# Small matrix products of two token mixers: HGRN scores gathered by tile width, meta blocks padded to full tiles, gated linear attention on blocks of 128 tokens

## The chip, the cores and the metric

The kernel runs on one core of a Trainium2 chip. The metric is device time in microseconds (us) of one execution, the median of three runs. Engines are named as in the profile: PE (TensorE matmul), PEld (its weight load), DVE (VectorE), ACT (ScalarE), POOL (GpSimd), SP (SyncE, which here only issues DMAs).

## The reference

Two transformer blocks run one after the other on 512 tokens of width 1024, all in float32. Both end in a gated feed-forward part of width 2816 with a short causal convolution. Ahead of that, the first block mixes tokens by gated linear attention (GLA, 4 heads of 128), a short convolution and sliding-window attention (SWA); the second, which has 16 learned meta tokens in front, by HGRN2 (8 heads of 128) and a Mamba-2 scan. The change touches GLA, HGRN2 and one transposition in Mamba-2.

GLA, per head, in chunks of 64 tokens (q, k already projected):

```python
b = jnp.cumsum(log_a, axis=2)                       # inside a chunk
attn = einsum('bnihk,bnjhk->bnhij', q * exp(b - b_ref), k * exp(b_ref - b))   # causal
o_intra = einsum('bnhij,bnjhv->bnihv', attn, v)
kv = einsum('bnjhk,bnjhv->bnhkv', k * exp(b_last - b), v)
state = exp(b_last) * state + kv                    # from chunk to chunk
o_inter = einsum('bnihk,bnhkv->bnihv', q * exp(b), state_before)
```

HGRN2 has the same form in chunks of 16, with a forget gate f in place of exp(log_a) and k = 1 - f:

```python
scores = where(causal, einsum('bnhrk,bnshk->bnhrs', q * exp(bcum), k * exp(-bcum)), 0)
o = einsum('bnhrs,bnshv->bnrhv', scores, v) + o_inter
```

## The kernel before

The large products stream through PE without a break: a weight tile of 128x128 times activations of 512 columns (256, 258 or 264 columns where meta tokens are carried along), in three passes, because each float32 operand is held as an exact sum of two parts (XH and XL, wh and wl). They write the PSUM tile `acc`. ACT (line 82) and DVE (line 83) make wh and wl of every eight weight tiles.

The token mixers are "small work" in three lanes: generators that are stepped after every k-step of the stream (`tick`). A `yield n` asks for n ticks before the next step. Their products write the PSUM tile `sm` and stand in PE's one queue between the large products; PE takes its queue in order. Which large products they stand between was set when the program was built, and is shown below where it changes. A float32 product of the mixers is two PE instructions ("passes") in the profile, a transposition one.

A product uses the part of the array that its operands need. The profile writes this as rows*columns: 128*128 is the whole array, 128*32 a product with 32 columns of weights, 32*128 one with 32 rows in the sum. Products that lie in different rows or columns of the array can be in flight side by side.

HGRN, `hg_head` and `hg_back`: the 528 tokens of a head are a meta block of 32 (16 zeros, 16 meta tokens) and four blocks of 128. Scores of a 128-block come in three steps: the whole block with factors taken relative to each sub-block of 32 (Km, Qm; in the profile `Qm,hb`), then two 32x32 corrections between neighbouring sub-blocks (K32, Q32), then a 64x64 correction (K64, Q64), each of which overwrites its part of PSUM. The `yield`s are at block level, so all of a head's score products are issued in one step. Then K and V are transposed to tokens (kt, vt), states S are summed (`kt` times `vt`, decays on DVE), outputs are at (scores) times vt plus Q1 times S, and the normed output `on` is transposed back. The meta block is a product with 32 rows (kt, vt, at0, on0). In Mamba-2's `z_gen`, the meta rows of `xtm` are transposed as a 16-row tile.

GLA, `gla_head`: chunks of 64 are paired into blocks of 128 columns. q1, k2 give the scores of a block (mask `glam` cuts it to two chunks); k4 is transposed to tokens; seven chunk products with 64 rows give seven states; outputs are at times v plus q3 times the state before, per chunk of 64.

Of the kernel before, what the change touches and what calls it, by code (L numbers as in the profile page):

```python
# [9 lines left out]
F32 = mybir.dt.float32  # L10
# [89 lines left out]
class Lane:  # L100
    """Small work that runs beside the stream of large matrix products."""
# [25 lines left out]
class Builder:  # L127
# [162 lines left out]
    def spread(self, cols, dst, pos=0):  # L290
        """cols: list of [n,1] token columns -> dst[:, pos:...] the same on all partitions."""
# [12 lines left out]
    def setup(self):  # L304
# [5 lines left out]
        cm = c.tile([P, 5 * P + 16], F32, name="cm")  # L310
        self.four = cm[:, 5 * P:]
        self.ident, self.le, self.gt, self.glam, self.ones = (cm[:, i * P:(i + 1) * P] for i in range(5))
# [30 lines left out]
    def swa(self, pool, sq, sk, svt):  # L343
        """Heads 0..3 live on the partitions 0..63, heads 4..7 on 64..127: one of each runs side by side."""
# [59 lines left out]
    def gla_head(self, pool, h, q, k, sgr):  # L404
# [25 lines left out]
        yield 8  # L430
# [4 lines left out]
        nc.vector.copy_predicated(at, self.glam.bitcast(U32).unsqueeze(1).to_broadcast([P, 4, P]), a4(ps))  # L435
        ebl = pool.tile([P, 8], F32, tag="ebl", name="ebl", bufs=2)
        nc.vector.tensor_copy(ebl, c3(q3)[:, :, 63])
        self.mul(k4, k4, k)
        self.mul(q3, q3, q)
# [7 lines left out]
        Ss = [None] + [None] * 7  # L447
        Sa, Sb = t2("q1"), pool.tile([P, 3, P], F32, tag="S", name="S", bufs=1)
        pks = [self.sm(), self.sm()]
        for n in range(7):  # L450
            blk, r = n // 2, (n % 2) * 64
            pk = pks[n % 2][:, n // 2 * P:(n // 2 + 1) * P]
            self.mm(pk, k4T[r:r + 64, blk * P:(blk + 1) * P], self.GVt[r:r + 64, blk, h * P:(h + 1) * P])
            Ss[n + 1] = a4(Sa)[:, n, :] if n < 4 else Sb[:, n - 4, :]
        for n in range(7):
            pk = pks[n % 2][:, n // 2 * P:(n // 2 + 1) * P]
            if n == 0:
                nc.vector.tensor_copy(Ss[1], pk)
            else:
                self.stt(Ss[n + 1], Ss[n], ebl[:, n:n + 1], pk, ALU.mult, ALU.add)  # L460
            if n == 3:
                yield 2
        yield 3
        po = self.sm()
        for n in range(8):
            blk, r = n // 2, (n % 2) * 64
            vb = self.GVt[:, blk, h * P:(h + 1) * P]
            if blk == 0:
                self.mm(po[r:r + 64, 0:P], at[:, 0, r:r + 64], vb, start=True, stop=r == 0)
            elif r == 0:  # L470
                self.mm(po[:, blk * P:(blk + 1) * P], at[:, blk, :], vb, start=True, stop=False)
            if n:
                self.mm(po[r:r + 64, blk * P:(blk + 1) * P], q3[:, n * 64:(n + 1) * 64], Ss[n], start=False, stop=True)
# [358 lines left out]
    def to_tokens(self, c, dst):  # L832
        """c [128, L] features -> dst [128, 5, 128] tokens, block 0 the meta tokens."""
# [88 lines left out]
    def hg_head(self, hp, h, f, hv, st, prev, back):  # L922
# [65 lines left out]
        p3 = ps.rearrange("p (a b) -> p a b", a=4)  # L988
        for i in range(4):
# [5 lines left out]
        at, at0 = self.hat, self.hat0  # L995
# [4 lines left out]
        ps0 = self.sm()  # L1000
        self.mm(ps0[0:32, 0:32], Km[:, 0:32], Qm[:, 0:32])
        nc.vector.copy_predicated(at0, self.le[0:32, 0:32].bitcast(U32), ps0[0:32, 0:32])
        self.mul(c3(Q1), c3(Qm), bc(fq, 17, 32))
        yield 1
        vt, kt = hp.tile([P, 5, P], F32, tag="hvt", name="hvt"), hp.tile([P, 5, P], F32, tag="hkt", name="hkt")
# [18 lines left out]
    def hg_back(self, hp, h, at, at0, Q1, kt, vt, tot, st):  # L1024
# [23 lines left out]
        nc.gpsimd.memset(ss, 0.0)  # L1048
        on, on0 = hp.tile([P, T], F32, tag="hon", name="hon"), hp.tile([32, P], F32, tag="hon0", name="hon0")
        self.act(on0, po0[0:32, 0:P], AF.Square, accum=ss[0:32, 0:1])  # L1050
# [6 lines left out]
        self.ts(on0, po0[0:32, 0:P], r[0:32, 0:1], ALU.mult)  # L1057
# [4 lines left out]
        self.tr(ps0[:, 0:32], on0, 32)  # L1062
# [6 lines left out]
    def block2(self, sqh, sqg):  # L1069
# [5 lines left out]
        def norm2():  # L1075
# [4 lines left out]
            # 1/sqrt(s2 r1^2 / D + EPS) r1 = 1/sqrt(s2 / D + EPS / r1^2)  # L1080
# [19 lines left out]
        with ExitStack() as sy:  # L1100
# [26 lines left out]
            with tc.tile_pool(reuse_waits="tile", name="m2", bufs=1) as mp:  # L1127
                xtm = mp.tile([P, 5, D], F32, name="xtm")
                Cs = [mp.tile([P, L], F32, name=f"mC{g}") for g in range(2)]
# [61 lines left out]
                def z_gen(j):  # L1191
# [8 lines left out]
                    self.tr(ps0[:, 0:META], xtm[0:META, 0, j * P:(j + 1) * P], META)  # L1200
# [68 lines left out]
            with tc.tile_pool(reuse_waits="tile", name="hp", bufs=1) as hp:  # L1269
# [6 lines left out]
                self.hat0 = hp.tile([32, 32], F32, name="hat0")  # L1276
                for a in (self.hat, self.hat0):
# [119 lines left out]
    def rms_spread(self, acc, dim, R, pos):  # L1397
        """acc [128, 2 + 512] sums of squares -> R[:, pos:...] the factor per column."""
# [10 lines left out]
def np_consts():  # L1409
# [4 lines left out]
    glam = le & (i[:, None] // 64 == i[None, :] // 64)  # L1414
    cm = np.concatenate([ident, le, gt, glam, np.ones((P, P)), i[:, None] % 32 == i[:16]], 1).astype(np.float32)
# [84 lines left out]
```

## Time and profile before

| what | us |
|---|---|
| three runs | 1825.75, 1828.38, 1829.14; median 1828.38 |
| profiled execution, first to last instruction (span) | 1825.3 |
| PE busy in the span | 1795.8 (98%) |
| DVE, ACT, POOL busy | 1120.1 (61%), 703.4 (39%), 173.1 (9%) |

The profile tells the span of its execution; the time of that execution lies a little above it, and the three runs lie 0.5 to 3.8 us above the span. Busy time of PE is a sum of intervals whose ends are modelled, so 98% says that something was always in flight, not that PE worked at its best pace. A row of the timeline merges like instructions that follow each other: its first number is the start of the first, and the distance from one row's start to the next tells what a group really cost.

### The profile page before, as it was taken

What the parts mean: (1) busy time and instruction counts of PE and PEld (TensorE: products, weight loads), DVE (VectorE), ACT (ScalarE), POOL (GpSimd) and SP (SyncE); (2) the same over time, 40 slices, a digit from 0 to 9 for tenths busy, and PEclk for the clock granted to TensorE, in tenths of its full rate; (3) what the DMA queues carried; (4) which work ended last, traced back from release to release, by engine and by line L of the source; (5) the groups of instructions that cost most, each with busy time, mean ns of one, the idle gap of its engine ahead of it and who ended that gap; (6) DMA issues with size and microseconds to landing.
All of it is one profiled execution on the core that took longest, in us unless ns stands there. A gap on an engine that the chain in (4) does not pass through costs nothing. (4 is left out here: it accounts for less than half of the span.)

```text
span 1825.3 us, 26947 instructions
## 1 busy us (share of the span) xinstructions
PE 1795.8 (98%) x11012; PEld 1559.1 (85%) x11012; DVE 1120.1 (61%) x1946; ACT 703.4 (39%) x1097; POOL 173.1 (9%) x231
## 2 busy tenths in 40 slices
PE   8999999999999999999999999999999999999997
PEld 6777778888888888888988889999999999999875
DVE  5476774444467777533698787666643577777332
ACT  5355342222344444333443334544432344444221
POOL 2000000000200000011154640000001000000000
PEclk9999999999999999999998999999999999999998
DMA  5221223233232223232211122121223233232222
GB/s 182 81 81 47 81 70 93 93 99 98 92 93 93 93 93 96 96 97 93 73 60 46 59 64 70 50 79 59 70 70 93 93 93 93 93 91 91 94 84 69
DMA packets 43451, 153.55 MB, mean 84 GB/s; under 512 B 5024, under 2 KB 5168, under 8 KB 43328
## 3 DMA queue, kind: packets, MB, share of 16 engines
q1 hardware_dynamic: 42480, 149.83, 26.1%
q8 instruction: 86, 1.41, 0.3%
q0 software_dynamic: 560, 1.74, 0.3%
q14 instruction: 37, 0.30, 0.1%
q10 hardware_dynamic: 288, 0.27, 0.0%
HBM read 149.72 MB, written 2.10 MB: 83 GB/s over the span
## 5 line engine op out<-in xcount | busy, mean ns | idle before, releaser
L179 PE MATMUL acc<-XH,wh 128*128 128x512 f32 (+3 forms) x2320 | 636.5, 328 | 0.0
L179 PE MATMUL acc<-XH,wl 128*128 128x512 f32 (+3 forms) x2320 | 620.7, 321 | 0.0
L179 PE MATMUL acc<-XL,wh 128*128 128x512 f32 (+3 forms) x2320 | 620.6, 321 | 0.0
L82 ACT CAST wh<-wraw 128x1024 fp32r<-128x1024 f32 (+1 forms) x279 | 291.9, 1046 | 538.9 <-PE acc L179 473.8
L83 DVE TENSOR_TENSOR wl<-wraw,wh 128x1024 fp32r<-128x1024 f32 (+1 forms) x279 | 343.2, 1230 | 214.5 <-ACT wh L82 207.0
L179 PEld LDWEIGHTS acc<-XH,wh 128*128 128x128 f32 x2320 | 385.9, 189 | 45.0 <-issue 8.8
L179 PEld LDWEIGHTS acc<-XH,wl 128*128 128x128 f32 x2320 | 385.9, 189 | 35.7 <-issue 1.8
L179 PEld LDWEIGHTS acc<-XL,wh 128*128 128x128 f32 x2320 | 386.3, 189 | 34.0 <-issue 0.9
L179 PE MATMUL acc<-FH,wh 128*128 128x512 f32 x352 | 140.5, 399 | 0.0
L179 PE MATMUL acc<-FH,wl 128*128 128x512 f32 x352 | 139.1, 395 | 0.0
L179 PE MATMUL acc<-FL,wh 128*128 128x512 f32 x352 | 138.2, 393 | 0.0
L162 DVE SCALAR_TENSOR_TENSOR c<-u,par_t,c 128x512 f32<-128x512 f32 x176 | 131.8, 749 | 6.8 <-ACT c L176 3.7
L150 DVE TENSOR_TENSOR u<-acc,R 128x512 f32<-128x512 f32 (+2 forms) x132 | 63.8, 510 | 90.1 <-PE acc L179 87.1
L334 POOL TENSOR_TENSOR sqa<-sqa,sqt 128x512 f32<-128x512 f32 x27 | 40.9, 1516 | 745.7 <-ACT sqt L176 745.7
L179 PEld LDWEIGHTS acc<-FH,wl 128*128 128x128 f32 x352 | 66.1, 188 | 16.8
L179 PEld LDWEIGHTS acc<-FL,wh 128*128 128x128 f32 x352 | 66.1, 188 | 15.7
L179 PEld LDWEIGHTS acc<-FH,wh 128*128 128x128 f32 x352 | 66.1, 188 | 14.9
L176 ACT ACTIVATE FH<-c 128x512 fp32r<-128x512 f32 x44 | 27.8, 632 | 116.3 <-DVE c L150 116.3
L150 DVE TENSOR_TENSOR H<-H,acc 128x512 f32<-128x512 f32 (+2 forms) x41 | 22.6, 568 | 77.8 <-PE acc L179 77.8
L176 ACT ACTIVATE c<-u,par_t 128x512 f32<-128x512 f32 x88 | 67.8, 770 | 2.2 <-DVE u L150 2.2
L176 ACT ACTIVATE c<-c 128x512 f32<-128x512 f32 x44 | 27.8, 632 | 85.7 <-DVE c L162 85.7
L179 PE MATMUL acc<-yh,wh 128*128 128x256 f32 (+1 forms) x256 | 51.5, 283 | 0.0
(388 smaller groups left out, 2087.4 us busy)
## 6 DMA issues: line engine op xcount, KB each, us to landing
wraw<-in_wts SPq DMA_DIRECT2D x277, 512.0 KB, 3.5
H<-in_xT SPq DMA_DIRECT2D x8, 256.0 KB, 9.0
out<-H SPq DMA_DIRECT2D x7, 256.0 KB, 2.7
wraw<-in_wts SPq DMA_DIRECT2D x2, 256.0 KB, 4.4
cm<-in_cm POOLq DMA_DIRECT2D x1, 328.0 KB, 5.7
r<-in_r POOLq DMA_DIRECT2D x1, 272.0 KB, 3.8
par_t<-in_par POOLq DMA_DIRECT2D x1, 256.0 KB, 4.0
r<-in_r POOLq DMA_DIRECT2D x1, 256.0 KB, 6.8
```

The costliest lines, as they stand in the source:

```text
L82: self.nc.scalar.copy(h[:, e], t[:, e])
L83: self.nc.vector.tensor_tensor(out=l[:, e], in0=t[:, e], in1=h[:, e].bitcast(F32), op=ALU.subtract)
L150: self.nc.vector.tensor_tensor(out=out, in0=a, in1=b, op=op)
L162: self.nc.vector.scalar_tensor_tensor(out=out, in0=a, scalar=s, in1=b, op0=op0, op1=op1)
L176: self.nc.scalar.activation(out=out, in_=a, func=func, scale=scale, **kw)
L179: self.nc.tensor.matmul(out, lhsT, rhs, start=start, stop=stop)
L334: self.nc.gpsimd.tensor_tensor(out=acc, in0=acc, in1=t, op=ALU.add)
```

## The change

Four edits. (1) HGRN scores: the four whole blocks first, then the eight 32x32 corrections, then the 64-corrections, each cut into two products with 32 columns of weights and 64 columns of data, so that all corrections have the width 128*32; the meta block's 32x32 product comes right behind. (2) Meta blocks are zero-padded to 128 rows: kt, vt, at0, on0 and the meta block of xtm are full tiles whose unused rows POOL zeroes once; the products and transpositions on them are 128*128. (3) GLA runs on blocks of 128: k4 and q3 are scaled by the decay of the neighbouring chunk, a separate product of 64x64 fills the scores between the two chunks of a block, three kv products of 128 rows replace seven of 64, three states seven, and seven output products of 128 replace twelve. (4) The mask glam is dropped from the constants. Comments and docstrings are removed too.

```diff
@@ gla_head
+        ebl = pool.tile([P, 12], F32, tag="ebl", name="ebl", bufs=2)
+        nc.vector.tensor_copy(ebl[:, 0:8], c3(q3)[:, :, 63])
+        e2 = ebl[:, 0:8].rearrange("p (n a) -> p n a", a=2)
+        eb = ebl[:, 8:12]
+        self.mul(eb, e2[:, :, 0], e2[:, :, 1])
+        self.mul(k4, k4, k)
+        self.mul(q3, q3, q)
+        yield 6
         ps = self.sm()
         for n in range(4):
             self.mm(ps[:, n * P:(n + 1) * P], k2[:, n * P:(n + 1) * P], q1[:, n * P:(n + 1) * P])
+        for n in range(4):
+            self.mm(ps[0:64, n * P + 64:(n + 1) * P], k4[:, n * P:n * P + 64], q3[:, n * P + 64:(n + 1) * P])
+        h2 = lambda t, a: t.rearrange("p (n a c) -> p n a c", a=2, c=64)[:, :, a, :]
+        self.mul(h2(k4, 0), h2(k4, 0), e2[:, :, 1:2].to_broadcast([P, 4, 64]))
+        self.mul(h2(q3, 1), h2(q3, 1), e2[:, :, 0:1].to_broadcast([P, 4, 64]))
...
-        for n in range(7):
-            blk, r = n // 2, (n % 2) * 64
-            pk = pks[n % 2][:, n // 2 * P:(n // 2 + 1) * P]
-            self.mm(pk, k4T[r:r + 64, blk * P:(blk + 1) * P], self.GVt[r:r + 64, blk, h * P:(h + 1) * P])
...
+        for n in range(3):
+            self.mm(pk[:, n * P:(n + 1) * P], k4T[:, n * P:(n + 1) * P], self.GVt[:, n, h * P:(h + 1) * P])
+        nc.vector.tensor_copy(S[:, 0, :], pk[:, 0:P])
+        for n in (1, 2):
+            self.stt(S[:, n, :], S[:, n - 1, :], eb[:, n:n + 1], pk[:, n * P:(n + 1) * P], ALU.mult, ALU.add)
...
+        for n in range(4):
+            c = slice(n * P, (n + 1) * P)
+            self.mm(po[:, c], at[:, n, :], self.GVt[:, n, h * P:(h + 1) * P], start=True, stop=n == 0)
             if n:
-                self.mm(po[r:r + 64, blk * P:(blk + 1) * P], q3[:, n * 64:(n + 1) * 64], Ss[n], start=False, stop=True)
+                self.mm(po[:, c], q3[:, c], S[:, n - 1, :], start=False, stop=True)
@@ hg_head
         for i in range(4):
             self.mm(p3[:, i, :], sc(Km, i), sc(Qm, i))
+        for i in range(4):
             for g in range(2):
                 self.mm(p3[64 * g:64 * g + 32, i, 64 * g + 32:64 * g + 64], K32[:, 2 * i + g, :], Q32[:, 2 * i + g, :])
-            self.mm(p3[0:64, i, 64:128], K64[:, 2 * i:2 * i + 2, :].rearrange("p a b -> p (a b)"),
-                    Q64[:, 2 * i:2 * i + 2, :].rearrange("p a b -> p (a b)"))
+        for i in range(4):
+            for g in range(2):
+                self.mm(p3[32 * g:32 * g + 32, i, 64:128], K64[:, 2 * i + g, :],
+                        Q64[:, 2 * i:2 * i + 2, :].rearrange("p a b -> p (a b)"))
+        ps0 = self.sm()
+        self.mm(ps0[0:32, 0:32], Km[:, 0:32], Qm[:, 0:32])
@@ hg_back
         for i in range(4):
-            n = 32 if i == 0 else P
-            self.mm(pk[:, i * P:(i + 1) * P], kt[0:n, i, :], vt[0:n, i, :])
+            self.mm(pk[:, i * P:(i + 1) * P], kt[:, i, :], vt[:, i, :])
...
-            n = 32 if i == 0 else P
-            o = po0[0:32, 0:P] if i == 0 else po[:, (i - 1) * P:i * P]
-            self.mm(o, at0 if i == 0 else at[:, i - 1, :], vt[0:n, i, :], start=True, stop=i == 0)
+            o = po0[:, 0:P] if i == 0 else po[:, (i - 1) * P:i * P]
+            self.mm(o, at0 if i == 0 else at[:, i - 1, :], vt[:, i, :], start=True, stop=i == 0)
...
-        self.tr(ps0[:, 0:32], on0, 32)
+        self.tr(ps0[:, 0:P], on0)
@@ block2
+                nc.gpsimd.memset(xtm[:, 0, :], 0.0)
...
-                    self.tr(ps0[:, 0:META], xtm[0:META, 0, j * P:(j + 1) * P], META)
+                    self.tr(ps0[:, 0:P], xtm[:, 0, j * P:(j + 1) * P])
```

PE's queue in the second HGRN head, before the change (the last number is the size of the output; `Qm,hb` is a whole block or, as 32x32, the meta block; `q,k` are the corrections):

```order
L179 MATMUL acc<-XH,wl 128x258
L179 MATMUL sm<-Qm,hb 128x128
L179 MATMUL sm<-q_9173,k_9174 32x32 x2
L179 MATMUL sm<-q_9175,k_9176 64x64
L179 MATMUL sm<-Qm,hb 128x128
...
L179 MATMUL sm<-Qm,hb 32x32
L179 MATMUL acc<-XH,wh 128x256
```

The first three `sm` rows stand four times, once for each block, so the width changes three times in each. After the change, at the same place:

```order
L179 MATMUL acc<-XH,wl 128x258
L179 MATMUL sm<-Qm,hb 128x128 x4
L179 MATMUL sm<-q_9147,k_9148 32x32 x8
L179 MATMUL sm<-q_9149,k_9150 32x64 x8
L179 MATMUL sm<-Qm,hb 32x32
L179 MATMUL acc<-XH,wh 128x256
```

The width now changes once on the way in and once on the way out, and there are four more products.

PE's queue at the outputs of the third GLA head before the change (`GVt,attnT` is at times v, `q,b` and `S,b` are the state times q3):

```order
L179 MATMUL sm<-GVt,attnT_162 64x128 x2
L179 MATMUL sm<-q_1833,b 64x128
L179 MATMUL sm<-GVt,attnT_162 128x128
L179 MATMUL sm<-q_1833,b 64x128 x2
L179 MATMUL sm<-GVt,attnT_162 128x128
L179 MATMUL sm<-q_1833,b 64x128
L179 MATMUL sm<-S,b 64x128
L179 MATMUL sm<-GVt,attnT_162 128x128
L179 MATMUL sm<-S,b 64x128 x2
```

After the change, from the scores of the same head on (`q,k` with a product of 128x128 are the scores, `b,la` is the new product between chunks, `cm,la` transposes k4, `GVt,a` is kv; "..." stands for 9, 6 and 9 large products):

```order
L179 MATMUL sm<-q_1707,k_1708 128x128 x4
L179 MATMUL sm<-b,la 64x64 x4
...
L182 MATMUL sm<-cm,la 128x128 x4
...
L179 MATMUL sm<-GVt,a_1791 128x128 x3
...
L179 MATMUL sm<-GVt,attnT_162 128x128 x2
L179 MATMUL sm<-q_1799,b 128x128
L179 MATMUL sm<-GVt,attnT_162 128x128
L179 MATMUL sm<-q_1799,b 128x128
L179 MATMUL sm<-GVt,attnT_162 128x128
L179 MATMUL sm<-q_1799,b 128x128
```

Everything but `b,la` has the full width now; `b,la` stands between two full-width groups.

## Rows read from the trace of the kernel before

**Rows 1.** The page: span, and PE's busy time.

```profile
span 1825.3 us, 26947 instructions
PE 1795.8 (98%) x11012; PEld 1559.1 (85%) x11012; DVE 1120.1 (61%) x1946; ACT 703.4 (39%) x1097; POOL 173.1 (9%) x231
```

**Rows 2.** What PE waited for: us in total, times, longest us.

```profile
PE sm L182 <- POOL xtm L918: 1.1, 1, 1.1
```

**Rows 3.** Windows: length, busy us of PE, PEld, DVE, ACT, POOL, clock, DMA.

```profile
200.00:400.00 200.00, 199.85 (x912) 159.35 (x911) 114.26 (x171) 68.81 (x98) 0.10 (x1) 1.00 0.28 89
...
900.00:1000.00 100.00, 92.45 (x658) 84.36 (x657) 90.00 (x146) 36.84 (x64) 43.63 (x43) 0.93 0.17 54
...
1200.00:1300.00 100.00, 100.00 (x828) 94.47 (x826) 63.39 (x177) 45.83 (x97) 3.69 (x19) 1.00 0.21 64
```

**Rows 4.** Timeline of PE (start us, us, instruction), scores of GLA's third head.

```profile
212.99 0.39 PE L179 MATMUL acc<-XH,wl 128*128 128x512 f32 x1
213.22 1.05 PE L179 MATMUL sm<-q,k 128*128 128x128 f32 x8
...
214.34 0.40 PE L179 MATMUL acc<-XL,wh 128*128 128x512 f32 x1
```

**Rows 5.** Timeline of PE, scores of one HGRN head.

```profile
1226.62 0.41 PE L179 MATMUL acc<-XH,wl 128*128 128x264 f32 x2
...
1227.62 0.49 PE L179 MATMUL sm<-Qm,hb 128*128 128x128 f32 x2
1228.04 0.51 PE L179 MATMUL sm<-q,k 128*32 128x32 f32 x6
...
1230.73 0.41 PE L179 MATMUL acc<-XL,wh 128*128 128x264 f32 x2
```

**Rows 6.** Timeline of PE, two halves of an SWA output.

```profile
153.48 0.32 PE L179 MATMUL sm<-pT,svt 128*64 128x128 f32 x1
153.49 0.32 PE L179 MATMUL sm<-pTb,svt 128*64 128x128 f32 x1
```

**Rows 7.** Timeline of PE, 16 passes of 64 columns in Mamba-2.

```profile
942.62 1.06 PE L179 MATMUL sm<-xdt,Lm 16*16 16x64 f32 x16
943.62 0.51 PE L179 MATMUL acc<-XH,wh 128*128 128x264 f32 x2
```

**Rows 8.** Timeline of PE, around the state products of one HGRN head.

```profile
1234.74 0.40 PE L179 MATMUL acc<-XL,wh 128*128 128x264 f32 x2
1234.98 0.40 PE L179 MATMUL acc<-XH,wl 128*128 128x264 f32 x2
...
1236.75 0.40 PE L179 MATMUL acc<-XL,wh 128*128 128x264 f32 x2
```

**Rows 9.** Timeline of PE, around the output products of that head.

```profile
1239.18 0.41 PE L179 MATMUL acc<-XH,wl 128*128 128x256 f32 x2
...
1241.98 0.40 PE L179 MATMUL acc<-XL,wh 128*128 128x256 f32 x2
```

**Rows 10.** Timeline of PE, around the transpositions of that head's output.

```profile
1251.65 0.40 PE L179 MATMUL acc<-XH,wl 128*128 128x256 f32 x2
...
1252.95 0.40 PE L179 MATMUL acc<-XL,wh 128*128 128x256 f32 x2
```

**Rows 11.** Timeline of PE, around kv of GLA's third head.

```profile
217.83 0.39 PE L179 MATMUL acc<-XH,wl 128*128 128x512 f32 x1
...
219.58 0.39 PE L179 MATMUL acc<-XL,wh 128*128 128x512 f32 x1
```

**Rows 12.** Timeline of PE, around the outputs of that head.

```profile
222.60 0.39 PE L179 MATMUL acc<-XH,wl 128*128 128x512 f32 x1
...
226.21 0.39 PE L179 MATMUL acc<-XL,wh 128*128 128x512 f32 x1
```

**Rows 13.** The page's groups: a DVE product and a POOL sum of 512 columns.

```profile
L334 POOL TENSOR_TENSOR sqa<-sqa,sqt 128x512 f32<-128x512 f32 x27 | 40.9, 1516 | 745.7 <-ACT sqt L176 745.7
...
L150 DVE TENSOR_TENSOR H<-H,acc 128x512 f32<-128x512 f32 (+2 forms) x41 | 22.6, 568 | 77.8 <-PE acc L179 77.8
```

More of the change, by code (lines that the diff above doesn't have):

```diff
@@ L309, in setup @@
         self.par_t = c.tile([P, NPAR], F32, name="par_t")
-        cm = c.tile([P, 5 * P + 16], F32, name="cm")
-        self.four = cm[:, 5 * P:]
-        self.ident, self.le, self.gt, self.glam, self.ones = (cm[:, i * P:(i + 1) * P] for i in range(5))
+        cm = c.tile([P, 4 * P + 16], F32, name="cm")
+        self.four = cm[:, 4 * P:]
+        self.ident, self.le, self.gt, self.ones = (cm[:, i * P:(i + 1) * P] for i in range(4))
         nc.scalar.preload_act_table_set("exp_and_others")
@@ L429, in gla_head @@
         self.act(q3, b, AF.Exp, scale=1.0 / 16)
-        yield 8
+        yield 2
+        ebl = pool.tile([P, 12], F32, tag="ebl", name="ebl", bufs=2)
[6 more added lines that the diff above has]
+        yield 6
         ps = self.sm()
@@ L446, in gla_head @@
         yield 2
-        Ss = [None] + [None] * 7
-        Sa, Sb = t2("q1"), pool.tile([P, 3, P], F32, tag="S", name="S", bufs=1)
-        pks = [self.sm(), self.sm()]
-        for n in range(7):
-            blk, r = n // 2, (n % 2) * 64
-            pk = pks[n % 2][:, n // 2 * P:(n // 2 + 1) * P]
-            self.mm(pk, k4T[r:r + 64, blk * P:(blk + 1) * P], self.GVt[r:r + 64, blk, h * P:(h + 1) * P])
[L454 to L462, printed above, removed]
+        S, pk = a4(t2("q1")), self.sm()
+        for n in range(3):
[3 more added lines that the diff above has]
+            self.stt(S[:, n, :], S[:, n - 1, :], eb[:, n:n + 1], pk[:, n * P:(n + 1) * P], ALU.mult, ALU.add)
         yield 3
         po = self.sm()
[L465 to L471, printed above, removed]
+        for n in range(4):
+            c = slice(n * P, (n + 1) * P)
+            self.mm(po[:, c], at[:, n, :], self.GVt[:, n, h * P:(h + 1) * P], start=True, stop=n == 0)
             if n:
-                self.mm(po[r:r + 64, blk * P:(blk + 1) * P], q3[:, n * 64:(n + 1) * 64], Ss[n], start=False, stop=True)
+                self.mm(po[:, c], q3[:, c], S[:, n - 1, :], start=False, stop=True)
         ss = pool.tile([P, 4], F32, tag="ss", name="ss", bufs=2)
@@ L999, in hg_head @@
         nc.vector.copy_predicated(at, self.le.bitcast(U32).unsqueeze(1).to_broadcast([P, 4, P]), p3)
-        ps0 = self.sm()
-        self.mm(ps0[0:32, 0:32], Km[:, 0:32], Qm[:, 0:32])
-        nc.vector.copy_predicated(at0, self.le[0:32, 0:32].bitcast(U32), ps0[0:32, 0:32])
+        nc.vector.copy_predicated(at0[0:32, 0:32], self.le[0:32, 0:32].bitcast(U32), ps0[0:32, 0:32])
         self.mul(c3(Q1), c3(Qm), bc(fq, 17, 32))
         yield 1
-        vt, kt = hp.tile([P, 5, P], F32, tag="hvt", name="hvt"), hp.tile([P, 5, P], F32, tag="hkt", name="hkt")
+        vt, kt = self.hvt, self.hkt
         def to_tok(src, dst):
@@ L1047, in hg_back @@
         ss = hp.tile([P, 5], F32, tag="hss", name="hss", bufs=2)
-        nc.gpsimd.memset(ss, 0.0)
-        on, on0 = hp.tile([P, T], F32, tag="hon", name="hon"), hp.tile([32, P], F32, tag="hon0", name="hon0")
-        self.act(on0, po0[0:32, 0:P], AF.Square, accum=ss[0:32, 0:1])
+        on, on0 = hp.tile([P, T], F32, tag="hon", name="hon"), hp.tile([P, P], F32, tag="hon0", name="hon0")
+        self.act(on0, po0[:, 0:P], AF.Square, accum=ss[:, 0:1])
         for i in range(4):
@@ L1056, in hg_back @@
                  bc(r[:, 1:5], 4, P))
-        self.ts(on0, po0[0:32, 0:P], r[0:32, 0:1], ALU.mult)
+        self.ts(on0, po0[:, 0:P], r[:, 0:1], ALU.mult)
         yield 11
@@ L1275, in block2 @@
                 self.hat = hp.tile([P, 4, P], F32, name="hat")
-                self.hat0 = hp.tile([32, 32], F32, name="hat0")
-                for a in (self.hat, self.hat0):
+                self.hat0 = hp.tile([P, P], F32, name="hat0")
+                self.hvt, self.hkt = hp.tile([P, 5, P], F32, name="hvt"), hp.tile([P, 5, P], F32, name="hkt")
+                for a in (self.hat, self.hat0, self.hvt[:, 0, :], self.hkt[:, 0, :]):
                     nc.gpsimd.memset(a, 0.0)
@@ L1413, in np_consts @@
     gt = (i[:, None] > i[None, :])
-    glam = le & (i[:, None] // 64 == i[None, :] // 64)
-    cm = np.concatenate([ident, le, gt, glam, np.ones((P, P)), i[:, None] % 32 == i[:16]], 1).astype(np.float32)
+    cm = np.concatenate([ident, le, gt, np.ones((P, P)), i[:, None] % 32 == i[:16]], 1).astype(np.float32)
     dist = P + i[:, None] - np.arange(256)[None, :]
@@ L1473 @@
 IN_SHAPES = {
-    "xT": (P, KD, T), "metaT": (P, KD, META), "par": (P, NPAR), "cm": (P, 5 * P + 16), "dist": (P, 256),
+    "xT": (P, KD, T), "metaT": (P, KD, META), "par": (P, NPAR), "cm": (P, 4 * P + 16), "dist": (P, 256),
     "r64": (P, T), "r32": (P, PADL), "r4": (P, 17), "wal": (P, T), "wts": (NCH, P, 1024), "wga": (P, KD, 32), "wdt": (P, KD, 32),
```

8 lines of the change are left out of this document (2 added, 6 removed).

## The prediction

> **What bounds the kernel now.** I read the page first. PE has something in flight for 1795.8 of the 1825.3 us [rows 1], and DVE, the next engine, is busy for 61%. So time can only come from PE: from instants in which it waits, or from work that costs it more than it should. The list of waits is short and the windows say why: in the two stretches that the change touches most, GLA (inside 200 to 400 us) and HGRN (inside 1200 to 1300 us), PE is busy for 199.85 of 200 and 100.00 of 100 us at a clock of 1.00, with DVE at 57% and 63% [rows 3]. Only Mamba-2, ahead of HGRN, is different: from 900 to 1000 us DVE is busy for 90 us, PE stands still for 7.5, and the granted clock is 0.93, that is, the lower of its two levels (1.2 instead of 2.4 GHz) for 14 of the 100 us.
>
> Then the timeline, since a busy PE hides how dear a block of small products is. I measure a block by starts: from the large-product row ahead of it to the second one behind it (the first one behind still pays for the way out), less two rows of the undisturbed stream, which follow each other by 0.23 us for one 512-column product [rows 4] and 0.24 us for a pair of 256 to 264 columns [rows 8].
>
> A block whose products all have the width of the stream is cheap: GLA's scores, eight passes of 128*128, cost 214.34 - 212.99 - 0.46 = 0.89 us, or 0.11 a pass [rows 4]. HGRN's scores have the same eight full passes plus 26 small ones and cost 1230.73 - 1226.62 - 0.48 = 3.63 us [rows 5]. The difference is not the small passes' size. Inside that block a full product that stands between narrow ones takes 1228.04 - 1227.62 = 0.42 us instead of 0.22 [rows 5]: each change of width leaves PE about 0.1 us without progress before and after. There are 13 such changes in a head.
>
> One rule speaks against this reading. The Trainium skill, "TensorE: Matmul & The Clock Gate", section "Part 3: Packing small matmuls — row/col tiling", says that a weight load overlaps products in flight only when its rows of the array differ. By that rule full-width passes behind each other would pay load and product in turn, 0.21 each as at a change of width; the scores' saving below would fall by 8 x 0.10 = 0.8 us a head, no padded block would gain, and the sum would be 12 us at most instead of 27.6. The eight passes at 0.11 [rows 4] contradict it here, so the sum goes by the row.
>
> **The change, part by part.**
>
> HGRN scores, eight heads. What remains: eight full passes, 0.88. One way into the narrow width and one out, which together cost what I read above for entering and leaving once, 0.2, plus the slower first large product, 0.1: 0.3. Then 16 passes 32 by 32, 16 passes of 32 weight columns on 64 data columns, and two for the meta block. The two products of a pair lie in different columns of the array, and such pairs do go side by side: SWA's halves start 0.01 apart [rows 6]. For a pass of 64 columns the nearest row is Mamba-2's, 1.00 us for 16, or 0.06 [rows 7], so eight rounds of pairs are 0.48. For 32 columns the bounds are 0.03 (half of that) and 0.06 (no faster); I take 0.04: eight rounds 0.32, the meta block 0.08. Sum 0.88 + 0.3 + 0.88 = 2.06, a saving of 1.57 a head, **12.6** in all. Best case (0.03 and 0.05): 1.75 a head. Worst case, if the pairs go one after the other: 34 passes at 0.05 to 0.06 are 1.86, the block 3.04, and the saving 0.59 a head, 4.7 in all.
>
> Padded state products: 1236.75 - 1234.98 - 0.48 = 1.29 now [rows 8]; eight full passes are 0.88. Saving 0.41 x 8 = **3.3**. Padded outputs: 1241.98 - 1239.18 - 0.48 = 2.32 now [rows 9]; 18 full passes are 1.98. Saving 0.34 x 8 = **2.7**. Transposing the output back: 1252.95 - 1251.65 - 0.48 = 0.82 now [rows 10]; five at 0.11 are 0.55. Saving 0.27 x 8 = **2.2**. The eight transpositions of xtm have the same form. The first four lie ahead of a wait of 1.1 us for POOL's sum of xtm [rows 2], and that sum does not depend on them: what they save comes back as a longer wait there. The last four save 4 x 0.27, say **1.0**.
>
> GLA, four heads. kv: 219.58 - 217.83 - 0.46 = 1.29 now [rows 11]; six full passes are 0.66, saving 0.63. Outputs: 226.21 - 222.60 - 0.46 = 3.15 now, 24 passes with eight changes of width [rows 12]; 14 full passes are 1.54, saving 1.61. The new product between chunks adds a way in and out, 0.3, and eight passes of 64 weight and 64 data columns, which the trace does not show at full rows; I take 0.06 [rows 7] rather than the 0.11 of a full pass [rows 4], since such a pass loads and streams half as much: 0.78 (up to 1.2). Net 0.63 + 1.61 - 0.78 = 1.46, **5.8** in all.
>
> Off PE. DVE gets two half-size products and one tiny one in each GLA head and loses four of its state sums: nothing, as a 512-column product is 0.57 us [rows 13] and DVE has over 40% free. The transposition of k4 now needs one of the half-size products, which itself waits for the new product on PE. Nine large products, 2.1 us, lie between in the third head's queue; without them the wait would be some 0.5 us a head. POOL's zeroing of xtm, 1024 columns, stands in its queue ahead of Mamba-2's first memsets. POOL is nearly idle there, and a sum of 512 columns takes it 1.5 us [rows 13], so it is hidden behind the large products of the first projection; uncovered, up to 3 us once. The other three zeroings are an eighth of that each. The shorter constant and the eight dropped memsets of five columns count for nothing: neither is waited for.
>
> Sum: 12.6 + 3.3 + 2.7 + 2.2 + 1.0 + 5.8 = 27.6 us. The profiled execution spans 1825.3 us and the three runs lie 0.5 to 3.8 above that; 27.6 off their median, 1828.38, gives **1801 us**. A measurement of this kernel can tell about 0.2%, 3.7 us, from no change.
>
> **The rivals.**
>
> *Small passes in single file.* The 34 narrow passes of an HGRN head stand in one burst now, and the rows that show pairs side by side have 128 columns a pass. If PE cannot start short passes faster than one in 0.05 to 0.06 us, HGRN's scores save 4.7 instead of 12.6, and the time is 1809. For it: the shortest even pace in any row is 0.06 [rows 7]. Against it: the pair's 0.01 us between starts [rows 6]. Chance 0.15. The same skill page ("Wait — 56ns, not 53.3ns?") has such a rule: where the sequencer decodes matmuls in software, it spends about 62 ns on each, and that becomes the bound for short ones; by it 34 passes are 2.1 us, the block 3.3, and the time 1811. No run here shows which decoder is at work.
>
> *The saving turns into waits.* A head of HGRN takes some 32 us and loses 2.6; DVE's 63% [rows 3] becomes 69%, not a bound, but its chain from scores to transposed output, or GLA's shortened distances in the queue, could be late. If half is lost: 1815. In both windows PE is busy throughout today [rows 3]. Chance 0.08.
>
> *It ends slower.* Place: the transposition of k4 in each GLA head, with all large products queued behind it. DVE's half-size product stands behind whatever DVE is doing when PE finishes the product between chunks. At four heads this decides only from 27.6 / 4 = 6.9 us a head, on top of the 2.1 of cover; at 9 us a head the time is 1837. DVE is busy 57% there [rows 3] and a 512-column product takes it 0.57 us [rows 13], so it would need a backlog of a dozen and more. Chance 0.03.
>
> *The change does not do what it says.* If the lost 0.1 us at a width change were a wait for data, it would move along with the products: HGRN saves nothing, GLA only what ten fewer output passes take, 1.1 us a head, and the new product takes most of that back. Time 1825 to 1828. Against it: the same loss shows in three kinds of products, with quite different data [rows 5, 8, 10]. Chance 0.04.
>
> **How the numbers follow.** My forecast has 0.70, for 1796 to 1806: the pair's pace (0.2 a head, 1.6 either way), the product between chunks (1.7 more), and Mamba-2's low clock, 14 us at half speed [rows 3], which follows waits that will now fall at other instants, 3 us either way. To hold eight in ten the range must take in the single file: 1794 to 1811. Faster by over 0.2%: the forecast, the single file and the lost half, 0.93. Within 0.2%: 0.04. Slower: 0.03.
>
> **What would show it.** The score block of an HGRN head from 3.63 to about 2.1 us, state products 0.9, outputs 2.0, transposition 0.55; GLA kv 0.7, outputs 1.55, scores with the new product 1.7; PE at 100 of 100 us in HGRN. A score block near 3.0 means single file; new waits of PE on DVE between 120 and 260 us, or a clock under 1.00 after 1100 us, would make me wrong.

## The result

The changed kernel takes 1801.75 us (median; 1800.66 to 1802.95), the kernel before 1828.76 us beside it; the ratio is 0.9855, with a 95% interval of 0.9841 to 0.9869. The forecast was 1801.0, its range 1794 to 1811.

The page of the changed kernel: span, and PE's busy time, as in [rows 1].

```profile
span 1799.0 us, 26982 instructions
PE 1767.2 (98%) x11036; PEld 1550.6 (86%) x11036; DVE 1116.0 (62%) x1942; ACT 703.6 (39%) x1097; POOL 174.6 (10%) x226
```

PE issues 24 passes more and has 28.6 us less in flight; the span is 26.3 us shorter. That is what a kernel looks like whose busy PE was partly not getting on.

The timeline of PE in the changed kernel, at the blocks of [rows 5, 8, 9, 10, 4, 11, 12] in this order, and in between ("..." also cuts the middle of a block; `GAt,wal` is the first product of GLA's third head):

```profile
1210.56 0.40 PE L179 MATMUL acc<-XH,wl 128*128 128x264 f32 x2
1210.80 1.05 PE L179 MATMUL sm<-Qm,hb 128*128 128x128 f32 x8
1211.78 0.89 PE L179 MATMUL sm<-q,k 128*32 128x32 f32 x32
1212.50 0.22 PE L179 MATMUL sm<-Qm,hb 128*32 128x32 f32 x2
1212.66 0.51 PE L179 MATMUL acc<-XH,wh 128*128 128x264 f32 x2
1213.01 0.40 PE L179 MATMUL acc<-XL,wh 128*128 128x264 f32 x2
...
1217.26 0.40 PE L179 MATMUL acc<-XH,wl 128*128 128x264 f32 x2
...
1218.64 0.40 PE L179 MATMUL acc<-XL,wh 128*128 128x264 f32 x2
...
1221.06 0.40 PE L179 MATMUL acc<-XH,wl 128*128 128x256 f32 x2
...
1223.54 0.40 PE L179 MATMUL acc<-XL,wh 128*128 128x256 f32 x2
...
1233.22 0.40 PE L179 MATMUL acc<-XH,wl 128*128 128x256 f32 x2
...
1234.24 0.40 PE L179 MATMUL acc<-XL,wh 128*128 128x256 f32 x2
...
197.61 0.59 PE L179 MATMUL sm<-GAt,wal 128*128 128x512 f32 x1
...
207.58 0.39 PE L179 MATMUL acc<-XH,wl 128*128 128x512 f32 x1
208.03 1.16 PE L179 MATMUL sm<-q,k 128*128 128x128 f32 x8
209.97 0.68 PE L179 MATMUL sm<-b,la 128*64 128x64 f32 x8 [0.79 <-DVE b L150]
210.58 0.50 PE L179 MATMUL acc<-XH,wh 128*128 128x512 f32 x1
210.92 0.40 PE L179 MATMUL acc<-XL,wh 128*128 128x512 f32 x1
...
214.41 0.39 PE L179 MATMUL acc<-XH,wl 128*128 128x512 f32 x1
...
215.54 0.39 PE L179 MATMUL acc<-XL,wh 128*128 128x512 f32 x1
...
217.16 0.40 PE L179 MATMUL acc<-XH,wl 128*128 128x512 f32 x1
...
219.19 0.39 PE L179 MATMUL acc<-XL,wh 128*128 128x512 f32 x1
```

By the prediction's own measure (row ahead to second row behind, less two rows of stream) these blocks now cost: HGRN scores 1213.01 - 1210.56 - 0.48 = 1.97, state products 0.90, outputs 2.00, transposing back 0.54; GLA's kv 0.67, outputs 1.57. All of them are where the prediction wanted them. Only GLA's scores with the new product are not: 2.88 in this third head, with a stall of 0.79 in the middle. In the first head, where PE does not wait, the same block runs from 131.94 to 134.11 and costs 1.71, as forecast. The other HGRN heads read like this one: 1.96 or 1.97 in heads two to eight, 3.62 to 3.64 before; the first head's block stands among other work and cannot be measured so.

PE's waits in the changed kernel, three of the list (us in total, times, longest):

```profile
PE sm L179 <- DVE b L150: 1.5, 2, 0.8
PE sm L182 <- DVE p L166: 1.3, 1, 1.3
PE sm L182 <- POOL xtm L913: 1.1, 1, 1.1
```

The row `DVE b` is new: PE waits for q3 times q, which only the new product reads so early. The wait for SWA's `p` was 0.59 before. The wait for POOL's xtm is as long as in [rows 2].

Windows (columns as in [rows 3]): the kernel before over GLA, then the changed kernel over GLA and over HGRN:

```profile
120.00:270.00 150.00, 148.47 (x829) 113.64 (x828) 113.85 (x232) 68.93 (x142) 0.40 (x4) 1.00 0.20 64
...
120.00:270.00 150.00, 146.46 (x805) 116.78 (x805) 111.48 (x230) 71.59 (x145) 0.40 (x4) 1.00 0.22 67
1100.00:1350.00 250.00, 249.51 (x2302) 247.63 (x2301) 170.36 (x464) 119.55 (x250) 11.60 (x37) 1.00 0.25 74
```

In HGRN PE stays busy (its only wait is 0.4 us for DVE's `hb` at the first head, which was there before) and DVE goes to 68%. In GLA PE now stands still for 3.5 of 150 us, at a clock of 1.00. It stood still for 1.5 before: the prediction's window for GLA, 200 to 400 us, holds only its last two heads.

Where the 26.3 us come from, by the starts of the same rows in the two traces: up to the first transposition of xtm the kernel gains 3.5 us (1005.32 to 1001.79), from there to HGRN's first score block, with the transpositions of xtm, 1.7 (1107.05 to 1101.79 is 5.3 in all), and from there to the end 21.0.

### The profile page after: what moved, and what is told of

It reads as the page before. It is cut to its first block, busy times and chain, and to the rows that moved or that the text cites. A ratio compares the mean times of both kernels' runs of the same rounds, so it can differ in the third digit from the quotient of the medians.

```text
span 1799.0 us, 26982 instructions
## 1 busy us (share of the span) xinstructions
PE 1767.2 (98%) x11036; PEld 1550.6 (86%) x11036; DVE 1116.0 (62%) x1942; ACT 703.6 (39%) x1097; POOL 174.6 (10%) x226
## 5 line engine op out<-in xcount | busy, mean ns | idle before, releaser
L179 PE MATMUL acc<-XH,wh 128*128 128x512 f32 (+3 forms) x2320 | 635.5, 328 | 0.0
L179 PE MATMUL acc<-XH,wl 128*128 128x512 f32 (+3 forms) x2320 | 621.2, 321 | 0.0
L179 PE MATMUL acc<-XL,wh 128*128 128x512 f32 (+3 forms) x2320 | 620.5, 321 | 0.0
L179 PEld LDWEIGHTS acc<-XH,wh 128*128 128x128 f32 x2320 | 385.9, 189 | 43.9 <-issue 8.5
L179 PEld LDWEIGHTS acc<-XH,wl 128*128 128x128 f32 x2320 | 385.8, 189 | 35.4 <-issue 1.5
L179 PEld LDWEIGHTS acc<-XL,wh 128*128 128x128 f32 x2320 | 386.7, 189 | 33.7 <-issue 0.5
L179 PE MATMUL acc<-FH,wh 128*128 128x512 f32 x352 | 140.6, 399 | 0.0
L179 PE MATMUL acc<-FH,wl 128*128 128x512 f32 x352 | 139.0, 395 | 0.0
L179 PE MATMUL acc<-FL,wh 128*128 128x512 f32 x352 | 138.3, 393 | 0.0
L150 DVE TENSOR_TENSOR u<-acc,R 128x512 f32<-128x512 f32 (+2 forms) x132 | 63.8, 510 | 90.1 <-PE acc L179 87.0
L179 PEld LDWEIGHTS acc<-FH,wl 128*128 128x128 f32 x352 | 66.1, 188 | 16.8
L179 PEld LDWEIGHTS acc<-FL,wh 128*128 128x128 f32 x352 | 66.1, 188 | 15.4
L179 PEld LDWEIGHTS acc<-FH,wh 128*128 128x128 f32 x352 | 66.1, 188 | 15.1
L150 DVE TENSOR_TENSOR H<-H,acc 128x512 f32<-128x512 f32 (+2 forms) x41 | 22.6, 569 | 77.8 <-PE acc L179 77.8
L179 PE MATMUL acc<-yh,wh 128*128 128x256 f32 (+1 forms) x256 | 51.5, 283 | 0.1
```

What stands on the lines that cost most here:

```text
L150: self.nc.vector.tensor_tensor(out=out, in0=a, in1=b, op=op)
L179: self.nc.tensor.matmul(out, lhsT, rhs, start=start, stop=stop)
```

## The experiments

**The three edits one at a time**, each put into the kernel before.

First the score products of `hg_head`, gathered and split as in the change:

```diff
+        for i in range(4):
             for g in range(2):
                 self.mm(p3[64 * g:64 * g + 32, i, 64 * g + 32:64 * g + 64], K32[:, 2 * i + g, :], Q32[:, 2 * i + g, :])
-            self.mm(p3[0:64, i, 64:128], K64[...], Q64[...])
+        for i in range(4):
+            for g in range(2):
+                self.mm(p3[32 * g:32 * g + 32, i, 64:128], K64[:, 2 * i + g, :], Q64[...])
```

> The kernel before with the new order of HGRN's score products alone. Theory (each change of width costs PE about 0.1 us on either side, the edits add up): each head's score block falls by the 1.66 us that the changed kernel's trace shows, 13.3 us in eight heads, about 1815.5 us. Rival (the parts lean on each other: with the meta products still narrow, PE meets new waits or the saving shrinks): the block falls by clearly less than 1.66, and the time is above 1819.

Measured: 1814.41 us against 1828.57, ratio 0.9924 (0.9912 to 0.9936), 14.2 us less. The score block costs the same as in the changed kernel, with all meta products still narrow. Then the padding, everywhere as here:

```diff
-            self.mm(pk[:, i * P:(i + 1) * P], kt[0:n, i, :], vt[0:n, i, :])
+            self.mm(pk[:, i * P:(i + 1) * P], kt[:, i, :], vt[:, i, :])
...
-                    self.tr(ps0[:, 0:META], xtm[0:META, 0, j * P:(j + 1) * P], META)
+                    self.tr(ps0[:, 0:P], xtm[:, 0, j * P:(j + 1) * P])
```

> The kernel before with the zero-padding of the meta blocks alone (kt, vt, at0, on0, xtm), old score order, old GLA. Theory: state products 0.39, outputs 0.31, transposing back 0.26 less per head, 7.6 in eight heads; xtm eight times 0.25, of which about 0.2 goes into a longer wait: together 9.4, about 1819.3 us. Rival (as the prediction had it: the first four transpositions of xtm are swallowed by the wait for POOL): 1.0 less saved, the wait for xtm longer by 1.0, about 1820.3; by the clock alone these two cannot be told apart, by the wait's row they can.

Measured: 1818.61 us, 0.9948 (0.9936 to 0.9960), 10.0 us less. PE's wait for POOL's xtm is 1.1 us, unchanged. The prediction's step is refuted: the first four transpositions of xtm kept most of their saving. The trace of the changed kernel shows why. POOL's sum starts when DVE's product `yt` ends, and that stands in DVE's queue among evacuations which follow PE: 1071.57 us before, 1067.30 after, 4.27 earlier, by exactly as much as PE's own row ahead of that block (1072.00 to 1067.73). The sum moved along with PE. From the first transposition of xtm to HGRN's first score the kernel with padding alone takes 100.4 us (1007.46 to 1107.88), the kernel before 102.2 (1005.59 to 1107.75): 1.7 us less, of the 8 x 0.26 = 2.1 that the blocks save. Last, the whole hunk of `gla_head`, of which these lines matter here:

```diff
+        self.mul(q3, q3, q)
+        yield 6
...
+            self.mm(ps[0:64, n * P + 64:(n + 1) * P], k4[:, n * P:n * P + 64], q3[:, n * P + 64:(n + 1) * P])
```

> The kernel before with GLA on blocks of 128 alone. Theory (the blocks save 8.7 us, the new product costs 0.8 a head, and PE newly waits for the product of q3 on DVE in two heads, 1.5 us): 3.3 us less, about 1825.4 us, with a row of PE waiting for DVE b. Rival (the prediction's sum: no new wait): 5.8 us less, about 1823 us, no such row.

Measured: 1824.13 us, 0.9977 (0.9968 to 0.9985), 4.4 us less; `PE sm L179 <- DVE b L150` is there with 1.5 us in two heads. The time lies between the two expectations; the row decides for the new wait. The three parts add up to 28.6 us where the whole change gives 26.8, each known to about 2 us, so times alone cannot tell whether the edits lean on each other. For HGRN the traces can: from its first score to its last transposition of an output it takes 240.0 us before, 226.2 with the scores alone, 232.4 with the padding alone and 218.8 in the changed kernel. That is 13.7 and 7.6 less, and 21.2 together: there they do not.

**What gathering is worth, and what splitting.** First the 64-corrections whole again, but gathered.

```diff
-                self.mm(p3[32 * g:32 * g + 32, i, 64:128], K64[:, 2 * i + g, :], ...)   # 8 products, 32 columns
+            self.mm(p3[0:64, i, 64:128], K64[:, 2 * i:2 * i + 2, :]..., ...)            # 4 products, 64 columns
```

> The changed kernel with the 64-corrections whole again (64x64), but still gathered: full blocks, 32-corrections and meta, 64-corrections. Theory (what pays is the gathering; the split only spares a change of width): three changes of width a head instead of two, 8 passes of 64 columns of weights instead of 16 of 32, so 0.1 to 0.2 us more a head, 1802.5 to 1803.5 us. Rival (the split into equal widths is what pays): most of the 1.66 a head comes back, above 1810 us.

Measured: 1802.46 us (1800.69 to 1802.72), ratio to before 0.9855 (0.9840 to 0.9870), not to be told from the changed kernel by its time. Its timeline at one score block:

```profile
1211.82 0.40 PE L179 MATMUL acc<-XH,wl 128*128 128x264 f32 x2
...
1214.43 0.41 PE L179 MATMUL acc<-XL,wh 128*128 128x264 f32 x2
```

The block costs 2.13 us, 0.16 more than in the changed kernel. So of the 1.66 us a head the gathering gives 1.5, and the split into one width 0.16, 1.3 us in all. Then the opposite: one width, but block by block.

```diff
         for i in range(4):
             self.mm(p3[:, i, :], sc(Km, i), sc(Qm, i))
-        for i in range(4):
             for g in range(2):
                 self.mm(... K32 ...)
-        for i in range(4):
             for g in range(2):
                 self.mm(... K64 ...)
```

> The changed kernel, same products with the same two widths, but block by block as before the change: full, four narrow pairs' products, full, and so on, so eight changes of width a head instead of two. Theory (each change of width costs; 1.66 us for eleven fewer changes is 0.15 each): 6 x 0.15 = 0.9 us more a head, 7.2 in eight heads, about 1809 us. Rival (only the number of different widths matters, or the split itself saves): about 1802 us, the score block as in the changed kernel.

Measured: 1809.58 us, 0.9896 (0.9883 to 0.9910), 7.8 us above the changed kernel. Its timeline at one score block:

```profile
1216.89 0.40 PE L179 MATMUL acc<-XH,wl 128*128 128x264 f32 x2
1217.13 0.38 PE L179 MATMUL sm<-Qm,hb 128*128 128x128 f32 x2
1217.44 0.36 PE L179 MATMUL sm<-q,k 128*32 128x32 f32 x8
1217.74 0.49 PE L179 MATMUL sm<-Qm,hb 128*128 128x128 f32 x2
1218.16 0.36 PE L179 MATMUL sm<-q,k 128*32 128x32 f32 x8
...
1220.28 0.41 PE L179 MATMUL acc<-XL,wh 128*128 128x264 f32 x2
```

The same products cost 2.91 us instead of 1.97: 0.94 for six more changes, 0.16 each, while 0.15 was expected. A full product between narrow ones takes 1218.16 - 1217.74 = 0.42 us again, as in [rows 5]. So over half of the 1.66 us that a score block gains is shown by taking back the order alone. The Trainium skill ("TensorEngine Tiling (Array Packing)", section "Key Properties") says that changing the tiling mode drains TensorE; the trace agrees, at 0.16 us a change.

One rival comes with this order: each correction now follows right behind the full product whose place in PSUM it overwrites, and PE could be waiting for that. The rows speak against it. Two full passes and the step into the narrow width take 1217.44 - 1217.13 = 0.31 us here. In the changed kernel, where three other blocks lie between a full product and its correction, eight full passes and the step take 1211.78 - 1210.80 = 0.98 us, which is 0.32 when six passes of 0.11 are taken off.

**Is it the side by side?** The prediction let the narrow products of a pair go side by side in different columns of the array. First their order was changed, so that neighbours share their columns.

```diff
-        for i in range(4):
-            for g in range(2):
+        for g in range(2):
+            for i in range(4):
                 self.mm(... K32 ...)      # the same for K64
```

> The changed kernel with the narrow products of one kind ordered so that neighbours lie in the same columns of the array: first the four with g = 0, then the four with g = 1. Theory (two products in different columns go side by side; in the same columns they go in single file at 0.05 to 0.06 us a pass): the 34 narrow passes take 1.8 instead of about 0.85 us, 0.9 a head, 7.5 in all, about 1809 us. Rival (short passes go at 0.025 us wherever they lie): no change, 1802 us.

Measured: 1803.87 us, 0.9864 (0.9851 to 0.9877), 2.1 us above the changed kernel: neither expectation. Its timeline at one score block:

```profile
1214.49 1.03 PE L179 MATMUL sm<-q,k 128*32 128x32 f32 x29
1215.31 0.22 PE L179 MATMUL sm<-Qm,hb 128*32 128x32 f32 x1
1215.36 0.22 PE L179 MATMUL sm<-q,k 128*32 128x64 f32 x1
1215.36 0.20 PE L179 MATMUL sm<-Qm,hb 128*32 128x32 f32 x1
1215.41 0.28 PE L179 MATMUL sm<-q,k 128*32 128x64 f32 x2
```

The meta product (`Qm,hb` behind the corrections) is the last in the program, yet it starts ahead of three passes of `q,k`. Products for other columns overtake those that wait for theirs, so this was no single file. The next kernel makes one, with every narrow product in the same 32 columns.

```diff
-                self.mm(p3[64 * g:64 * g + 32, i, 64 * g + 32:64 * g + 64], K32[...], Q32[...])
+                self.mm(p3[0:32, i, 32:64], K32[...], Q32[...])
-                self.mm(p3[32 * g:32 * g + 32, i, 64:128], K64[...], ...)
+                self.mm(p3[0:32, i, 64:128], K64[...], ...)
```

> The changed kernel with all narrow score products in the same 32 columns of the array (the second of each pair writes over the place of the first, so the scores are not the reference's). In the run with neighbours in the same columns, products that lie in other columns started ahead of earlier ones, so that was no single file; this is one. Theory (side by side is worth what the starts in one column show, 0.032 us a pass of 32 columns of data and 0.056 of 64): 16 x 0.032 + 16 x 0.056 + 0.06 = 1.47 us instead of 0.75 for the narrow passes, 0.7 a head, 5.7 in all, about 1807.5 us. Rival (the prediction's single file, 0.05 to 0.06 us for every pass): 1.1 a head, about 1810.5 us. Rival (columns do not matter): 1802 us.

Measured: 1807.75 us, 0.9888 (0.9871 to 0.9904), 6.0 us above the changed kernel. Its timeline at one score block:

```profile
1214.78 1.59 PE L179 MATMUL sm<-q,k 128*32 128x32 f32 x32
1216.20 0.23 PE L179 MATMUL sm<-Qm,hb 128*32 128x32 f32 x2
```

The 32 passes take 1216.20 - 1214.78 = 1.42 us in one column group and 1212.50 - 1211.78 = 0.72 in the changed kernel: side by side halves them, and is worth 0.70 us a head. It also shows that the prediction's single file was priced too high: 0.044 us a pass on average, not 0.05 to 0.06.

**The new wait in GLA.** The score products, with the new product behind them, come two ticks later.

```diff
         self.mul(q3, q3, q)
-        yield 6
+        yield 8
         ps = self.sm()
```

> The changed kernel with GLA's score products two ticks later (yield 8 in place of yield 6 behind the product of q3 on DVE). Theory (PE waited 0.79 and 0.69 us for that product because DVE had others ahead of it): both waits go, 1.5 us less, about 1800.3 us. Rival (the head as a whole is late, and the wait shows up again at the transposition of k4 or at the outputs): same time as the changed kernel, 1801.8, with a new row of PE waiting in 120 to 270 us.

Measured: 1798.83 us (1798.36 to 1799.75), 0.9835 (0.9822 to 0.9849), the fastest here, 2.9 us below the changed kernel. `DVE b` is gone from PE's waits, and `p` is short again; a small row comes for the half-size product ahead of k4's transposition:

```profile
PE sm L182 <- DVE p L166: 0.6, 1, 0.6
...
PE sm L182 <- DVE la L150: 0.2, 1, 0.2
```

Why the wait was there shows in DVE's timeline in the changed kernel, where PE is ready for the new product at 209.18:

```profile
207.96 0.69 DVE L150 TENSOR_TENSOR cy<-acc,R 128x512 f32<-128x512 f32 x1
...
208.63 0.69 DVE L150 TENSOR_TENSOR la<-la,kk 128x512 f32<-128x512 f32 x1
209.23 0.69 DVE L150 TENSOR_TENSOR b<-b,q 128x512 f32<-128x512 f32 x1
```

The product of q3 (`b<-b,q`) stands behind the other small work and an evacuation of the convolution (`cy`). Before the change only the outputs read it, three steps of the head later. In this third head there is a second cause: the scores themselves come nearer to the head's first product (`GAt,wal`), 208.03 - 197.61 = 10.4 us behind it. Before the change it was 213.22 - 200.52 = 12.7 us, by [rows 4] and this row of the kernel before:

```profile
200.52 1.02 PE L179 MATMUL sm<-GAt,wal 128*128 128x512 f32 x2
```

The missing 2.3 us are more than the 0.79 that PE waits, so at the old distance q3 would have been ready in time (an estimate from these rows). Why the scores come nearer is not shown: the `yield`s in between add up to 17 ticks in both kernels. With the two ticks the distance is 14.2 us (196.99 to 211.15). In the fourth head it is 12.8 us against 12.7 before, and the wait of 0.69 us there comes without this second cause. Two ticks mend both heads, so the two causes are not told apart by a run. Two ticks more in the remaining gaps were tried too:

```diff
# on top of yield 8
-        yield 3          # ahead of the transposition of k4
+        yield 4
-        yield 2          # ahead of kv
+        yield 3
```

> The version with GLA's scores two ticks later, and one tick more ahead of the transposition of k4 and ahead of kv. Theory (its two remaining waits of PE in GLA, 0.25 us for DVE's half-size product and 0.55 for ACT's copy, are only distances in the queue): both rows go, 0.8 us less, about 1798.0 us. Rival (each tick more moves a wait elsewhere): new rows of PE waiting in 120 to 270 us, 1798.8 us or more. The clock resolves hardly 0.8 us here; the rows of waits do.

Measured: 1799.96 us (1799.36 to 1800.50), 0.9844 (0.9830 to 0.9859). Both rows go (DVE's `la` and ACT's `a`, 0.2 and 0.5 us in the run before this one), and others come: `p` waits 1.5 us again and the outputs wait 0.4 for DVE's state:

```profile
PE sm L182 <- DVE p L166: 1.5, 1, 1.5
...
PE sm L179 <- DVE q L459: 0.4, 1, 0.4
```

The rival holds. Distances in this queue are not free to choose one by one.

**The new product at full width**, on top of the two ticks, so that GLA holds no narrow product of its own.

```diff
-            self.mm(ps[0:64, n * P + 64:(n + 1) * P], k4[:, n * P:n * P + 64], q3[:, n * P + 64:(n + 1) * P])
+            self.mm(px[:, n * 64:(n + 1) * 64], k4[:, n * P:(n + 1) * P], q3[:, n * P + 64:(n + 1) * P])
...
+        nc.scalar.copy(at[0:64, :, 64:128], px[0:64, 0:256].rearrange("p (a b) -> p a b", a=4))
```

> As the one with GLA's scores two ticks later, and the product between chunks at full width: 128 columns of weights, into a PSUM tile of its own, of which ACT copies the useful part over the scores; no narrow product is left in GLA. Theory (the new product's 0.8 us a head is mostly the way in and out): with eight passes at 0.06 the block is 0.3 us cheaper, 1.2 in four heads, about 1799 us; at 0.11 a pass it is 0.1 dearer, 1800.7. Rival (a pass of full rows costs its load whatever it streams, or the copy on ACT makes the outputs late): 1800.7 or more.

Measured: 1799.42 us (1798.71 to 1799.91), 0.9839 (0.9826 to 0.9853), no gain over the narrow form. The timeline of this kernel at the third head's scores:

```profile
211.19 0.39 PE L179 MATMUL acc<-XH,wl 128*128 128x512 f32 x1
...
212.31 1.00 PE L179 MATMUL sm<-b,la 128*128 128x64 f32 x8
213.12 0.48 PE L179 MATMUL acc<-XH,wh 128*128 128x512 f32 x1
213.43 0.40 PE L179 MATMUL acc<-XL,wh 128*128 128x512 f32 x1
```

Eight full-width passes on 64 columns of data take 0.81 us, 0.10 each; behind the first, their single starts lie 0.11 apart, as on 128 columns ([rows 4]). With 64 columns of weights they take 0.61 (209.97 to 210.58 in the changed kernel). What the narrow form loses at its two ends it wins back in its passes: 213.43 - 211.19 - 0.46 = 1.78 us for the block against 1.71, about the 0.1 us that the expectation gave for a pass of 0.11.

**Is every narrow row a change of width?** HGRN still has sixteen transpositions of the 32 meta tokens that the profile writes as 128*32. They were made full.

```diff
-            self.tr(ps[0:32, 0:P], src[:, 0:32])
+            self.tr(ps[:, 0:P], src[:, 0:P])
```

> The version with GLA's scores two ticks later, and in HGRN the transposition of the meta tokens of K and V at full width (128 columns read, the 32 useful rows copied): sixteen 128*32 transpositions less. Theory as the prediction put it (every change of width costs about 0.1 us on either side): 16 x 0.25 = 4.0 us less, about 1794.8 us. Rival (read from the changed kernel's trace, where these blocks of four full transpositions and one narrow one take as long as five full ones: a transposition of 32 columns is no change of width to PE): nothing, 1798.8 us.

Measured: 1799.31 us (1798.31 to 1800.07), 0.9841 (0.9826 to 0.9855): nothing gained. In the changed kernel this tile's transpositions, by shape (count, then ns least, median and most), are

```profile
L182 PE MATMUL sm<-cm,hk x30: 270/272/273, 1154.1 to 1302.9; 128*128 128x128 f32 x24, 128*32 128x128 f32 x6
```

and its blocks of four full and one 128*32 cost 1.03 us from the row ahead to the second row behind (1213.25 to 1214.28), the all-full ones here 1.04 (1212.23 to 1213.27). A transposition with fewer columns (32 here) is no change of width to PE; one with fewer rows was ([rows 10]: 0.82 us, now 0.54), and so are products with fewer columns.

## Why the prediction was right

The mechanism holds: a change of width costs PE time in which nothing gets on, and the gain comes from PE's blocks (in GLA also from 18 passes fewer a head in kv and outputs). By the prediction's terms, forecast against measured (count times the block's difference to [rows 5, 8, 9, 10]; xtm and GLA by the shift of starts):

| term | forecast, us | measured, us |
|---|---|---|
| HGRN scores | 12.6 | 8 x (3.63 - 1.97) = 13.3 |
| state products | 3.3 | 8 x (1.29 - 0.90) = 3.1 |
| outputs | 2.7 | 8 x (2.32 - 2.00) = 2.6 |
| transposing back | 2.2 | 8 x (0.82 - 0.54) = 2.2 |
| xtm | 1.0 | 1.7 |
| GLA, with the start | 5.8 | 3.5 |
| sum | 27.6 | 26.4 (spans: 26.3) |

*HGRN.* Right in mechanism and nearly in size: its four terms add up to 21.2 us, as much as the traces give from the first score to the last transposition of an output. The narrow passes and the meta block were assumed at 0.88 us ahead of the way out; with the way out they take 1212.66 - 1211.78 = 0.88. Side by side is needed for that, as assumed, but it is the smaller part: without it the block would still save 0.96 of its 1.66 us. The single-file rival, at either pace that was given for it, is answered by the 0.72 us for 32 passes, 0.0225 us each. By the rule that was weighed (the Trainium skill, "TensorE: Matmul & The Clock Gate", section "Part 3: Packing small matmuls — row/col tiling": a load overlaps only products in other rows) padding would have gained nothing; alone it gained 10.0 us, and the padded products go at 0.11 us a pass, so the rule, read this way, does not hold here.

*xtm.* The failed step is "what they save comes back as a longer wait there": the wait stayed at 1.1. What PE waited for depends on PE by way of DVE's queue.

*GLA.* kv and outputs saved 0.62 and 1.58 us a head, the new product cost 0.82: 5.5 in four heads, as forecast. The step that failed is "Off PE ... nothing". It looked at DVE's amount of work and at the transposition of k4, and not at the product of q3, which the change asks for several steps earlier, nor at the third head's scores, which come 2.3 us nearer to its start. That costs 1.17 us in the third head (2.88 against 1.71; 0.79 is the marked stall) and about 0.75 in the fourth, and the shifted queue 0.67 more at SWA's `p`: 2.6 of the 5.5. The prediction named new waits on DVE between 120 and 260 us as what would make it wrong. They came, but were small beside HGRN; of GLA's 3.5 us some 0.6 is not assigned. The other sign, a clock under 1.00 after 1100 us, shows only in the last 10 us of the program (0.97 over 1600 to 1800 us), where it was before (0.98 over 1600 to 1826). The rival that ends slower named the transposition of k4; no wait stands there in the changed kernel. What came is a small piece of the rival that the saving turns into waits, which named GLA's shortened distances.

So the sum is 1.2 us too high: GLA's 2.3 too many, against 1.1 too few in HGRN and xtm. That the forecast of the time came within 1 us is in part luck: two misses of opposite sign half cancel.

## What to carry to other kernels

Measure a block of small products from the row ahead to the second row behind: PE reads as busy while it changes width. Gather products of one width in each visit, and pad a lone small block that stands among full ones; but check which narrow rows really cost, since some do not, and a group of eight narrow passes came out even with the same group at full width. When an edit reads an operand earlier, look up when its engine made it before, however idle that engine is on average, and whether the edit moved the reader as well.

## What was not expected of the hardware

PE did not start all narrow products in program order: in the run with neighbours in the same columns, the meta product started about 0.1 us ahead of passes that stand before it. "PE takes its queue in order", in the section on the kernel before, is not quite so here. The Trainium skill ("TensorE: Matmul & The Clock Gate", section "Part 3: Packing small matmuls — row/col tiling") has matmuls start and end strictly in order; these starts differ from that.

In Mamba-2 a lower clock did not mean a longer stage. From 925 to 1005 us, the changed kernel and then the one with GLA two ticks later (the granted clock is the number behind POOL's):

```profile
925.00:1005.00 80.00, 72.33 (x491) 64.11 (x490) 69.83 (x92) 27.09 (x51) 43.67 (x38) 0.91 0.16 47
```

```profile
925.00:1005.00 80.00, 69.69 (x484) 61.45 (x484) 68.20 (x88) 27.25 (x50) 43.95 (x37) 0.94 0.15 47
```

In the first the clock is at its lower level for 13.7 us, in three stretches, in the second for 10.2 in one; yet from the product that waits for `xde` to the first transposition of xtm the first takes 68.2 us (933.87 to 1002.06) and the second 69.3 (931.65 to 1000.97). PE is busy for 72.33 instead of 69.69 us in the window: slower, it waits less for DVE. Why the stage is longer at the higher clock is not shown. The kernel before has 13.7 us at the lower level too, so the 26.3 us should hold none of this. But of the other runs, whose Mamba-2 code differs at most by the padding, some show one pattern and some the other, so spans that differ by 1 us say little here, and the rows of a block were used instead.
